# A two-layer decoder trunk with sparse attention on one core: blocks of queries of the first layer taken in the order 4, 5, 6, 7, 2, 3, 1, 0

## The chip, the cores and the metric

The kernel runs on one core of a Trainium2 chip. A core has a matrix engine (TensorE, PE in the profile, with its weight loads listed as PEld), VectorE (DVE), ScalarE (ACT), GpSimd (POOL) and SyncE (SP), which only issues transfers here. Each engine works through its own instructions in a fixed order and waits in place when an operand is not there. The metric is the device time of one execution in microseconds (us).

## The reference, cut to what matters

1,024 tokens of width 1,024 pass through two layers. In each, a modulated layer norm feeds one input projection, whose columns go to two branches: a gated spatial mixing (`u`, `v`, `z_a`) and an attention of 8 heads with one shared key and value, in which a small indexer scores all earlier keys and keeps 256 per query. Both branches go through one output projection, and a layer norm ends the layer.

```python
def hybrid_layer(x, cond, cos, sin, w_ada, b_ada, w_in, ..., w_out, ln_g, ln_b):
    h = layer_norm(x) * (1.0 + scale) + shift
    u, v, z_a, q, k, val, z_b, q_idx, k_idx, w_idx = jnp.split(h @ w_in, SPLIT_POINTS, axis=-1)
    y_a = jax.nn.silu(z_a) * spatial_gating_unit(u, v, v_norm_g, v_norm_b, w_spatial, b_spatial)
    ...
    y_b = jax.nn.silu(z_b) * sparse_attention(q, k, val, q_idx, k_idx, w_idx)
    y = jnp.concatenate([y_a, y_b], axis=-1) @ w_out
    return layer_norm(ALPHA * x + gate * y, ln_g, ln_b)
```

Attention is causal and goes by blocks of 128 queries, numbered 0 to 7. Block i sees (i + 1) x 128 keys at most, so block 7 has eight times the keys of block 0. The blocks do not depend on each other, and each gives 128 rows of the layer's output. The second layer needs all 1,024 rows for its keys, and 512 rows for each half of its projections.

## The kernel before, in words

A layer (`layer`, line 873 on) projects the tokens in two halves of 512, with weights on the sides as products of 128x512. Every float32 product is done as three products of split numbers: an array is split into a high part (ScalarE, L302) and a low part (GpSimd, L303). The list `self.halves` (L882) says which half of the tokens each projection takes first; the second layer takes it from the order of the layer before. After the first projections come the indexer's scores (`scores`, products L528, sums L535), then a bisection on VectorE that finds each query's 256th score (`select`, counting passes L543), interleaved with the other projections and with the spatial gating (`sgu`, L442 and L480, one step for each block of 128 tokens). `u_za` (L488 on) multiplies the gating result by the projected `u` and `z_a` on VectorE (L492), a half at a time.

Attention then runs over steps t = 0 to 15, two for each block (four heads each), in the order `ORDERS[l]` (L73). What stands beside it is bound to the *position* of a block in that order, not to its number:

- Step t: scores of the step (`att_soft`: products L678, VectorE L679, ScalarE exponent L684, GpSimd scaling by the reciprocal L687) and the product with the values of step t - 1 (`att_pv`: transposes L698, split on ScalarE and VectorE L701 and L702, products L703 and L704, sum L710).
- Between these products, `fill` sets products of the output projection (`out_mm`, L740), in pieces of three. 384 of them are in a layer. For positions 0 to 3 (`MERGE`) the gated branch's half (`merge_top`) and the attention's half (`out_bottom`) share an accumulator; for the last four positions the gated half comes early (`out_top` at t = 0, 1, 3, 5, stored in memory), and only the attention's half comes after the block.
- `out_bottom` of position k runs at t = 2k + 3. It ends with a layer norm and, on GpSimd, two passes over 128x1024 (L795, L796); only the last position does these on VectorE (`FAST`).
- The product of the attention with its gate (L712) stands on VectorE, but on GpSimd for blocks 1 and 5 (`ZPB`).
- Toward the next layer: `next_x` (from t = 7), `next_hT` (t = 9 for positions 0 and 1, t = 13 for positions 2 and 3; transposes L272, GpSimd L286), the first weights of the next layer (`first_load`, t = 16, with their splits on GpSimd), and `next_hT` of the last four positions after the loop.

So the number of the block decides only how much attention a step holds: 8 score products of 128x512 or less per four heads and two chunks for the long blocks, and i + 1 transposed groups in `att_pv`.

```python
        for t in range(-1, T + 2):
            ...
            if t >= 3 and t % 2 == 1:
                todo += [self.out_bottom(l, A[order[(t - 3) // 2]], wb, (t - 3) // 2 in self.FAST[l])]
            if t in self.TOPS[l] and self.TOPS[l].index(t) not in self.MERGE[l]:
                todo += [self.out_top(l, order[self.TOPS[l].index(t)], wt)]
            if t >= 2 and t % 2 == 0 and (t - 2) // 2 in self.MERGE[l]:
                todo += [self.merge_top(l, A[order[(t - 2) // 2]], wt)]
            if not last and t in self.NH:
                k = self.NH.index(t)
                todo += [self.next_hT(l + 1, order[k:k + self.NH.count(t)], self.HN)]
```

The order of each engine's instructions is set when the program is built, by a scheduler that moves independent work past each other; what it did is shown in the section on the change.

Of the kernel before, what the change touches and what calls it, by code (L numbers as in the profile page):

```python
# [66 lines left out]
class Trunk:  # L67
# [2 lines left out]
    PACE_SEL = 0.8  # L70
    STEPS = 6
    PTAGS = ('ya', 'w', 'w', 'ya', 'w')
    ORDERS = ((1, 0, 2, 3, 4, 5, 6, 7), (4, 5, 6, 2, 3, 7, 1, 0))  # L73
    PACE = 1.1
    RDVE = 1
    DMOD = ()
# [685 lines left out]
    def bottom_split(self, l, A):  # L762
        A["r"] = self.load_row(self.xin[l] if self.ORDERS[l].index(A["i"]) in self.MERGE[l] else self.r_dram[l], A["i"])
        A["ys"] = self.g("gc", [P, 4, P], F32R), self.g("gc", [P, 4, P], F32R)
        self.split(A["ys"][0], A["ys"][1], A["y"])
# [8 lines left out]
    def out_bottom(self, l, A, w, end):  # L774
        nc = self.nc
        i, r = A["i"], A["r"]
        for nh in range(2):
            acc = yield from self.out_mm(w, A["ys"], nh, A["acc"][nh])
            rv = r[:, nh * 512:(nh + 1) * 512]
            if self.ORDERS[l].index(i) in self.MERGE[l]:  # L780
                nc.vector.scalar_tensor_tensor(rv, rv, ALPHA, acc, op0=ALU.mult, op1=ALU.add)  # L781
# [94 lines left out]
    def layer(self, l, wts):  # L876
# [4 lines left out]
        self.ya = []  # L881
        self.halves = (0, 1) if l == 0 or self.ORDERS[l - 1][0] < 4 else (1, 0)  # L882
        specs = [(C_QI + 256, True, lambda w: self.queries(l, 1, 1, w))]
# [63 lines left out]
        nc.sync.dma_start(self.lb, a["ln_b"][l].partition_broadcast(P))  # L947
        order = self.ORDERS[l]
        steps = [(i, g) for i in order for g in range(2)]
# [111 lines left out]
```

## Time and profile before

| what | us |
|---|---|
| three runs | 1204.15, 1205.03, 1211.92 (median 1205.03) |
| profiled execution | 1208.58, of which the span of the trace is 1206.9 |
| first layer: up to the start of attention | 417 |
| first layer: attention and output projection | 417 to 651 |
| second layer: first projections, scores, rest of the projections | 651 to 993 |
| second layer: attention and output projection | 993 to 1199 |
| busy: PE, DVE, POOL, ACT | 1122.7 (93%), 842.1 (70%), 554.7 (46%), 502.2 (42%) |

The rows below are of the profiled execution. Times are from the start of the span. PEclk is the granted clock of TensorE, as a share of its higher level of 2.4 GHz: 1.00 is that level, 0.50 the lower level of 1.2 GHz. Matmuls overlap, so the busy time of one (some 0.4 us) is more than what it takes of the engine; the chain of work that ended last shows the latter.

### The profile page before, as it was taken

What the parts mean: (1) busy time and instruction counts of PE and PEld (TensorE: products, weight loads), DVE (VectorE), ACT (ScalarE), POOL (GpSimd) and SP (SyncE); (2) the same over time, 40 slices, a digit from 0 to 9 for tenths busy, and PEclk for the clock granted to TensorE, in tenths of its full rate; (3) what the DMA queues carried; (4) which work ended last, traced back from release to release, by engine and by line L of the source; (5) the groups of instructions that cost most, each with busy time, mean ns of one, the idle gap of its engine ahead of it and who ended that gap; (6) DMA issues with size and microseconds to landing.
All of it is one profiled execution on the core that took longest, in us unless ns stands there. A gap on an engine that the chain in (4) does not pass through costs nothing. (4 is left out here: it accounts for less than half of the span.)

```text
span 1206.9 us, 16501 instructions
## 1 busy us (share of the span) xinstructions
PE 1122.7 (93%) x5460; PEld 892.3 (74%) x5460; DVE 842.1 (70%) x1900; ACT 502.2 (42%) x972; POOL 554.7 (46%) x469
## 2 busy tenths in 40 slices
PE   5889999997999989988988999999989998999997
PEld 1467788866878778866766787888677886787885
DVE  6775666999773355688985467589977127878775
ACT  0342355420202454465764435562211136667561
POOL 1563310553323495474766532126323357565653
PEclk9989999998899989999999999999989998999999
DMA  8935721567412574322232474222621246132311
GB/s 264 278 101 179 205 71 36 166 219 257 117 54 79 166 218 158 105 97 62 86 95 74 138 229 123 70 68 88 227 90 45 88 132 202 51 106 88 114 36 61
DMA packets 127057, 152.11 MB, mean 126 GB/s; under 512 B 17396, under 2 KB 94580, under 8 KB 126968
## 3 DMA queue, kind: packets, MB, share of 16 engines
q1 hardware_dynamic: 126968, 151.03, 40.4%
q8 instruction: 43, 0.70, 0.2%
q14 instruction: 46, 0.38, 0.1%
HBM read 111.40 MB, written 35.40 MB: 122 GB/s over the span
## 5 line engine op out<-in xcount | busy, mean ns | idle before, releaser
L349 PE MATMUL pacc<-h,w 128*128 128x512 f32 (+2 forms) x2304 | 548.5, 394 | 10.8 <-DVE ya L492 8.4
L349 PEld LDWEIGHTS pacc<-h,w 128*128 128x128 f32 (+1 forms) x2304 | 427.1, 190 | 106.8 <-DVE ya L492 10.1
L303 POOL TENSOR_TENSOR w<-wr,w 128x512 fp32r<-128x512 f32 (+1 forms) x100 | 133.0, 1345 | 247.7 <-ACT w L302 231.9
L740 PE MATMUL pacc<-h,gc 128*128 128x512 f32 x768 | 196.7, 401 | 10.8 <-ACT gc L302 10.8
L740 PEld LDWEIGHTS pacc<-h,gc 128*128 128x128 f32 x768 | 143.8, 192 | 40.0 <-ACT gc L302 11.9
L302 ACT ACTIVATE w<-wr 128x512 fp32r<-128x512 f32 (+1 forms) x100 | 56.4, 601 | 208.9 <-PE pacc L349 147.0
L535 DVE SCALAR_TENSOR_TENSOR sc<-gc,wi,sc 128x384 f32<-128x384 f32 (+3 forms) x140 | 99.3, 752 | 38.8 <-ACT gc L530 37.0
L678 PE MATMUL ps<-kd,q 128*128 128x512 f32 (+4 forms) x384 | 106.2, 377 | 9.1 <-DVE mx L679 8.8
L702 DVE TENSOR_TENSOR ga<-ppt,ga 128x512 fp32r<-128x512 f32 x144 | 96.6, 684 | 15.5 <-ACT ga L701 14.9
L701 ACT ACTIVATE ga<-ppt 128x512 fp32r<-128x512 f32 x144 | 82.4, 592 | 36.8 <-PE ppt L698 35.9
L368 POOL TENSOR_TENSOR ga<-ga,ga 128x512 fp32r<-128x512 f32 (+2 forms) x40 | 56.9, 1429 | 85.5 <-ACT ga L367 76.8
L678 PEld LDWEIGHTS ps<-kd,q 128*128 128x128 f32 x384 | 65.1, 196 | 26.7 <-DVE mx L679 19.5
L687 POOL TENSOR_SCALAR w<-w,rd 128x256 f32<-128x256 f32 (+6 forms) x77 | 61.3, 799 | 50.7 <-DVE rd L686 32.5
L698 PE MATMUL ppt<-ident,w 128*128 128x128 f32 x349 | 74.9, 276 | 0.0
L239 POOL TENSOR_TENSOR rs<-rs,mhalf 128x1 f32<-128x1 f32 x48 | 34.8, 730 | 81.2 <-DVE rs L238 81.2
L722 DVE TENSOR_TENSOR wr<-wr,r 128x1024 f32<-128x1024 f32 x8 | 12.1, 1508 | 84.6 <-DMA wr<-in_w_out 52.3
L684 ACT ACTIVATE w<-w,mx 128x256 f32<-128x256 f32 (+6 forms) x77 | 60.6, 787 | 23.4 <-DVE mx L679 23.1
L703 PE MATMUL po<-ga,vv 128*128 128x512 f32 x144 | 62.4, 433 | 8.5 <-DVE gb L710 6.7
L543 DVE TENSOR_SCALAR_CACHE_REDUCE junkd<-sc,sv 128x384 int8<-128x384 f32 (+2 forms) x72 | 67.7, 940 | 1.4
L704 PE MATMUL po<-ga,vv 128*128 128x512 f32 x144 | 63.2, 439 | 3.0 <-DVE ga L702 2.9
L530 ACT ACTIVATE gc<-ppt 128x384 f32<-128x384 f32 (+3 forms) x96 | 47.9, 526 | 30.4 <-PE ppt L528 25.8
L199 DVE SCALAR_TENSOR_TENSOR r<-r,cond,r 128x1024 f32<-128x1024 f32 x28 | 41.8, 1494 | 25.4 <-DMA r<-in_w_ada 25.4
(198 smaller groups left out, 1750.5 us busy)
## 6 DMA issues: line engine op xcount, KB each, us to landing
wr<-in_w_in SPq DMA_DIRECT2D x50, 512.0 KB, 4.7
r<-in_w_ada SPq DMA_DIRECT2D x32, 512.0 KB, 4.2
q<-q SPq DMA_DIRECT2D x112, 128.0 KB, 3.2
q<-ga SPq DMA_DIRECT2D x48, 256.0 KB, 3.0
h<-in_w_ada SPq DMA_DIRECT2D x32, 256.0 KB, 5.2
wr<-in_w_out SPq DMA_DIRECT2D x16, 512.0 KB, 4.1
r<-r SPq DMA_DIRECT2D x14, 512.0 KB, 3.9
r<-x SPq DMA_DIRECT2D x12, 512.0 KB, 4.8
```

The costliest lines, as they stand in the source:

```text
L303: self.nc.gpsimd.tensor_tensor(lo, src, hi.bitcast(F32), op=ALU.subtract)
L349: self.nc.tensor.matmul(acc[:m, :tn], w[:, k, :m], h[:, k % 2, t0:t0 + tn], start=(k == 0 and i == 0), stop=(k == NK - 1 and i == 2))
L535: nc.vector.scalar_tensor_tensor(sc[:, c0:c0 + w], r[:, :w], wsc, sc[:, c0:c0 + w], op0=ALU.mult, op1=ALU.add)
L543: self.nc.vector.tensor_scalar(j[:, :n], sc, thr, None, op0=op, op1=ALU.add, accum_out=out)
L678: nc.tensor.matmul(ps[:, :w], q[:, g * 4 + h, :], self.KD[x][:, c0:c0 + w], start=(x == 0), stop=(x == 1))
L687: nc.gpsimd.tensor_scalar(pm[:, :n], pm[:, :n], rd, 0.0, op0=ALU.mult, op1=ALU.add)
L698: nc.tensor.transpose(pt[:, h * P:(h + 1) * P], pr[h][:, kt * P:(kt + 1) * P], self.ident)
L701: nc.scalar.activation(ph, pt, AF.Copy)
L702: nc.vector.tensor_tensor(pl, pt, ph.bitcast(F32), op=ALU.subtract)
L703: nc.tensor.matmul(o, self.V[:, kt, :], ph, start=(kt == 0), stop=False)
L704: nc.tensor.matmul(o, self.V[:, kt, :], pl, start=False, stop=(kt == i))
L740: self.nc.tensor.matmul(acc, s[:, k, :], m[:, cs], start=(first and k == i == 0), stop=(not more and k == 3 and i == 2))
```

## The change

The first layer's order of blocks is turned so that the long ones come first. Everything that is bound to a position stays at its position. Two things follow beside the order itself: `self.halves` of the second layer becomes (1, 0), since the first block of the order is not below 4, so that tokens 512 to 1023 are projected first there; and the last blocks to leave the first layer are 2, 3, 1 and 0, so tokens 0 to 511 are the later ones. The second layer's own order of attention stays. The counts of instructions stay on TensorE, VectorE, ScalarE and GpSimd.

```diff
@@ -70,7 +70,7 @@
     PTAGS = ('ya', 'w', 'w', 'ya', 'w')
-    ORDERS = ((1, 0, 2, 3, 4, 5, 6, 7), (4, 5, 6, 2, 3, 7, 1, 0))
+    ORDERS = ((4, 5, 6, 7, 2, 3, 1, 0), (4, 5, 6, 2, 3, 7, 1, 0))
```

The first place is GpSimd near the end of the first layer's attention. Names with `gc` are splits of an attention result on its way to L740, `ya_2280` and `ya_2282` are weights of the next layer, `r` are rows in the closing norm. Before:

```order
L239 TENSOR_TENSOR rs_2236_7393<-rs_2236_7393,mhalf_5_71 128x1
L239 TENSOR_TENSOR rs_2241_7409<-rs_2241_7409,mhalf_5_71 128x1
L795 TENSOR_TENSOR r_2175_7190<-r_2175_7190,r_1490_4947 128x1024
L303 TENSOR_TENSOR ya_2280_7538<-wr_2277_7533,ya_2279_7537 128x512
L303 TENSOR_TENSOR ya_2280_7538<-wr_2278_7535,ya_2279_7537 128x512
L796 TENSOR_TENSOR r_2175_7190<-r_2175_7190,r_1491_4948 128x1024
L303 TENSOR_TENSOR ya_2282_7544<-wr_2277_7533,ya_2281_7543 128x512
L303 TENSOR_TENSOR ya_2282_7544<-wr_2278_7535,ya_2281_7543 128x512
L303 TENSOR_TENSOR gc_2270_7510<-gb_2127_7046,gc_2269_7509 128x512
```

Now, from the scaling of the last probabilities of block 0 (L687) on:

```order
L687 TENSOR_SCALAR ya_2244_7423<-ya_2244_7423,rd_2249_7436 128x256
L795 TENSOR_TENSOR r_2141_7110<-r_2141_7110,r_1490_4947 128x1024
L712 TENSOR_TENSOR gb_2106_7015<-gb_2106_7015,gb_2105_7013 128x512
L303 TENSOR_TENSOR ya_2280_7538<-wr_2277_7533,ya_2279_7537 128x512
L303 TENSOR_TENSOR ya_2282_7544<-wr_2277_7533,ya_2281_7543 128x512
L796 TENSOR_TENSOR r_2141_7110<-r_2141_7110,r_1491_4948 128x1024
L303 TENSOR_TENSOR ya_2280_7538<-wr_2278_7535,ya_2279_7537 128x512
L303 TENSOR_TENSOR ya_2282_7544<-wr_2278_7535,ya_2281_7543 128x512
L303 TENSOR_TENSOR gc_2223_7363<-gb_2106_7015,gc_2222_7362 128x512
L303 TENSOR_TENSOR w_2369_8064<-wr_2366_8059,w_2368_8063 128x512
L303 TENSOR_TENSOR gc_2270_7510<-gb_2192_7287,gc_2269_7509 128x512
```

The split of the last block (`gc_2270`) is the last of these in both. What is new is that the split of the block before it (`gc_2223`, block 1) has moved behind the weights as well, and its gate product L712 stands on GpSimd ahead of it.

The second place is TensorE at the same point. Now, with block 1's output products (`pacc_2231`, `pacc_2247`) and the last transposes of block 0 (`ppt_2264`):

```order
L698 MATMUL ppt_2264_7491<-ident_4_66,w_2239_7406 128x128
L698 MATMUL ppt_2264_7491<-ident_4_66,ya_2244_7423 128x128
L272 MATMUL ppt_2296_7599<-ident_4_66,q_2224_7366 128x128
L272 MATMUL ppt_2298_7609<-ident_4_66,q_2224_7366 128x128
L272 MATMUL ppt_2300_7619<-ident_4_66,q_2224_7366 128x128
L740 MATMUL pacc_2231_7383<-h_1494_4956,gc_2222_7362 128x512
L740 MATMUL pacc_2231_7383<-h_1495_4957,gc_2222_7362 128x512
L740 MATMUL pacc_2247_7430<-h_1494_4956,gc_2222_7362 128x512
L740 MATMUL pacc_2247_7430<-h_1495_4957,gc_2222_7362 128x512
L703 MATMUL po_2263_7490<-ga_2265_7496,vv_144_599 128x512
L704 MATMUL po_2263_7490<-ga_2266_7497,vv_144_599 128x512
L740 MATMUL pacc_2231_7383<-h_1494_4956,gc_2223_7363 128x512
```

Before, the output products of the block ahead of the last (block 6, `gc_2177`) were over by then, and the last transposes of block 7 stood among transposes for the next layer (L272):

```order
L698 MATMUL ppt_2264_7491<-ident_4_66,w_2195_7241 128x128
L698 MATMUL ppt_2264_7491<-ident_4_66,ya_2201_7259 128x128
L704 MATMUL po_2242_7413<-ga_2260_7475,vv_144_599 128x512
L703 MATMUL po_2242_7413<-ga_2262_7485,vv_144_599 128x512
L272 MATMUL ppt_2296_7599<-ident_4_66,q_2178_7196 128x128
L272 MATMUL ppt_2296_7599<-ident_4_66,q_2238_7402 128x128
```

What moved is the whole of block 1's output projection, 24 products, to a place behind the last attention of the layer, where only the last block's 24 stood before.

The third place is VectorE in the second layer, at the gating (L480, whose four rows are one group of 128 tokens, the last group being `po_2674`) and the first products with `u` (L492, first of `pacc_2733`). Before:

```order
L480 SCALAR_TENSOR_TENSOR ya_2605_9007<-po_2642_9188,vg_2570_8773,bsum_2572_8777 128x128
L543 TENSOR_SCALAR junkd_2651_9232,sv_2603_8976<-sc6_2498_8551,sv_2603_8976 128x896
L243 TENSOR_SCALAR gc_2673_9320<-ppt_2669_9308,mv_2671_9315,rs_2672_9317 128x512
L492 TENSOR_TENSOR ya_2580_8806<-ya_2580_8806,pacc_2733_9707 128x512
L543 TENSOR_SCALAR junkd_2652_9234,sv_2603_8976<-sc7_2532_8654,sv_2603_8976 128x1024
```

Now:

```order
L480 SCALAR_TENSOR_TENSOR ya_2599_8947<-po_2674_9322,vg_2570_8773,bsum_2572_8777 128x128
L480 SCALAR_TENSOR_TENSOR ya_2605_9007<-po_2674_9322,vg_2570_8773,bsum_2572_8777 128x128
L585 TENSOR_SCALAR ps_2607_9034<-sv_2603_8976 128x6
L492 TENSOR_TENSOR ya_2580_8806<-ya_2580_8806,pacc_2733_9707 128x512
L492 TENSOR_TENSOR ya_2586_8866<-ya_2586_8866,pacc_2740_9770 128x512
```

The gating goes through its groups from token 0 up in both. The half of `u` that comes first now belongs to tokens 512 to 1023, so `pacc_2733` is used up only after the eighth group, where it was used up after the fourth.

## Rows read from the trace of the kernel before

**Rows 1.** Stages: us, busy (x instructions) of each engine, PEclk, DMA share, GB/s.
```profile
417.00:589.00 172.00, 158.27 (x779) 127.66 (x778) 126.73 (x358) 98.99 (x202) 106.88 (x96) 0.95 0.40 122
589.00:651.00 62.00, 54.36 (x273) 41.85 (x272) 45.59 (x102) 39.50 (x74) 45.29 (x39) 0.94 0.37 115
993.00:1199.00 206.00, 195.97 (x1005) 158.83 (x1003) 153.64 (x421) 121.08 (x242) 122.08 (x109) 0.98 0.31 96
```

**Rows 2.** Chain that ended last, second layer's attention: start, length in us, what.
```profile
1173.88 0.11 PE ppt L698
...
1175.36 5.48 PE pacc L740 x24
```

**Rows 3.** What TensorE waited for, 417 to 589: us in total, times, longest.
```profile
PE ps L678 <- DVE mx L679: 6.7, 11, 2.1
PE pacc L740 <- ACT gc L302: 3.1, 1, 3.1
```

**Rows 4.** The same view, 589 to 651.
```profile
PE po L703 <- DVE gb L710: 3.1, 2, 1.9
PE pacc L740 <- ACT gc L302: 2.6, 1, 2.6
```

**Rows 5.** The same view, 993 to 1199.
```profile
PE pacc L740 <- ACT gc L302: 5.1, 1, 5.1
```

**Rows 6.** Columns of rows 1, short stretches of the first layer's attention.
```profile
421.50:431.50 10.00, 6.85 (x23) 5.38 (x23) 5.34 (x19) 6.62 (x18) 9.19 (x8) 0.50 0.79 237
440.00:460.00 20.00, 20.00 (x99) 16.96 (x98) 11.73 (x36) 11.16 (x26) 13.90 (x14) 1.00 0.68 214
580.00:600.00 20.00, 18.74 (x101) 14.78 (x100) 19.62 (x46) 15.12 (x28) 16.66 (x14) 1.00 0.25 82
```

**Rows 7.** GpSimd by form, 417 to 651: count | busy us, mean ns | idle before.
```profile
L795 POOL TENSOR_TENSOR r<-r,r 128x1024 f32<-128x1024 f32 x7 | 17.4, 2491 | 4.5 <-ACT r L253 4.3
L796 POOL TENSOR_TENSOR r<-r,r 128x1024 f32<-128x1024 f32 x7 | 16.8, 2394 | 0.1
...
L303 POOL TENSOR_TENSOR gc<-gb,gc 128x512 fp32r<-128x512 f32 x8 | 10.4, 1294 | 7.8 <-ACT gc L302 7.8
...
L239 POOL TENSOR_TENSOR rs<-rs,mhalf 128x1 f32<-128x1 f32 x13 | 7.6, 597 | 5.8 <-DVE rs L238 5.7
...
L687 POOL TENSOR_SCALAR w<-w,rd 128x256 f32<-128x256 f32 x7 | 5.3, 756 | 0.0
L303 POOL TENSOR_TENSOR ya<-wr,ya 128x512 fp32r<-128x512 f32 x4 | 5.0, 1282 | 0.0
...
L687 POOL TENSOR_SCALAR ya<-ya,rd 128x256 f32<-128x256 f32 x6 | 3.8, 641 | 0.0
```

**Rows 8.** GpSimd in time near the tail: start, us, instructions [idle <- releaser].
```profile
605.14 2.81 POOL L795 TENSOR_TENSOR r<-r,r 128x1024 f32<-128x1024 f32 x1 [1.03 <-ACT r L253]
...
625.82 4.34 POOL L303 TENSOR_TENSOR w<-wr,w 128x256 fp32r<-128x256 f32 x6 [7.41 <-PE ppt L698]
...
633.00 2.38 POOL L795 TENSOR_TENSOR r<-r,r 128x1024 f32<-128x1024 f32 x1 [1.81 <-ACT r L253]
```

**Rows 9.** TensorE in time: ends of two out products; second layer's last score.
```profile
595.78 1.29 PE L740 MATMUL pacc<-h,gc 128*128 128x512 f32 x5
...
626.06 1.41 PE L740 MATMUL pacc<-h,gc 128*128 128x512 f32 x5
...
807.85 0.62 PE L528 MATMUL ps<-r,q 128*128 128x512 f32 x2
...
879.50 0.79 PE L349 MATMUL pacc<-h,w 128*128 128x512 f32 x1 [3.36 <-DVE ya L492]
```

**Rows 10.** VectorE in time, second layer: end of the scores.
```profile
813.21 0.17 DVE L557 BATCH_NORM_AGGREGATE smv<-bn 128x2 f32<-128x6 f32 x1
```

**Rows 11.** VectorE's lines, 810 to 880: count | busy us, mean ns | idle before.
```profile
L543 DVE TENSOR_SCALAR_CACHE_REDUCE junkd<-sc,sv 128x384 int8<-128x384 f32 (+5 forms) x24 | 22.5, 936 | 0.2
...
L364 DVE TENSOR_TENSOR ga<-ga,ga 128x512 f32<-128x512 f32 x3 | 2.5, 828 | 0.0
```

## The prediction, made before the changed kernel ran

> **What bounds the kernel now.** I read the stages first [rows 1]. In the first layer's attention, the stretch that the change rearranges, TensorE is busy 158.27 of 172 us and then 54.36 of 62; in the second layer's attention, 195.97 of 206. So TensorE bounds every stage, and the change leaves its counts alone. A new order can then gain or lose only idle time and granted clock. In the first piece these are 13.7 us idle and, at a clock of 0.95, 172 x 0.05 = 8.6 us; in the second, 7.6 and 62 x 0.06 = 3.7. For what an instruction takes of TensorE I went to the chain that ended last: 24 products of 512 columns in 5.48 us, so 0.228 each, and a transpose in 0.11 [rows 2]. Then the waits, stage by stage [rows 3 to 5], and GpSimd, which does the last step ahead of many of them [rows 7, 8].
>
> **The change part by part.** I cut the first layer's attention where the fourth position's output projection ends. In the new order that is block 7 and TensorE's row 2346; what stands ahead (matrix work of the four long blocks with the early output halves) comes to 144 us: 288 L740, 55 each of L703 and L704 at 0.228, 220 L698 and 12 L272 at 0.11, and 148 L678 by width. The first 172 us before hold nearly the same amount, 143.5 us by the same prices, so the two pieces can be compared one to one.
>
> *A, the opening, up to block 7's output products.* Before: 172 us for 143.5, so 28 us lost. Part of this belongs to the start of attention, which stays: in ten microseconds near its beginning the clock is 0.50, so 5.0 us are lost, with the DMA share at 0.79 [rows 6], and the single wait of 3.1 us for the first split [rows 3]. What remains is 13.7 - 3.1 = 10.6 us idle and 8.6 - 5.0 = 3.6 of clock, 14.2 together. The second layer's attention begins with 4, 5, 6 already, and loses there 10.0 - 5.1 [rows 1, 5] idle, or 4.1 for 172 us, and 0.02 x 172 = 3.4 of clock: 7.5. The difference is 14.2 - 7.5 = 6.7; I take **-6**. Bounds: 0 if the waits for VectorE [rows 3] only change place, -12 if nearly all of the 14.2 goes.
>
> *B, the tail: blocks 2 (its end), 3, 1 and 0 with the output products of the last four positions.* TensorE's own price is 44.4 us against 46.9 before, which took 62. But the small blocks have 2 to 4 transposed groups each, so TensorE reaches the end early, and it is GpSimd's fixed order that decides. The last products of block 1 read the low half `gc_2223`, which stands behind everything else on GpSimd. From block 7's first norm pass (L795) to that split, GpSimd has, at the rows' means [rows 7]: 3 pairs of L795 and L796 (2.49 + 2.39), 14.6; 16 scalings L687 of 256 wide at 0.70 (between 0.756 and 0.641), 11.2; 4 passes L286 for the next layer, of 128x512 like the splits and so at 1.29, 5.2; 5 L239 at 0.60, 3.0; 3 splits `gc` at 1.29, 3.9; the 6 small weight splits as one 4.34 piece [rows 8], 4.3; 4 splits `ya` at 1.28, 5.1; and block 1's L712, which has the split's 1.29 by its shape, 1.3. The sum is 48.6. In front of it lies the way from the last product of the bottom to L795: 597.07 to 605.14 is 8.1 and 627.47 to 633.00 is 5.5 [rows 8, 9]; I take 7. Behind it stand the 24 products of block 1, less the four that need only the high half, and the 24 of block 0: 44 x 0.228 = 10.0. GpSimd itself will wait for its inputs; its row shows such a wait of 1.0 and 1.8 us per norm [rows 8], I take 2 in all. While TensorE waits the clock falls, and I take 3.4, near the 3.7 that this stretch lost before. Sum: 7 + 48.6 + 2 + 10.0 + 3.4 = 71.0, against 62, so **+9**. Bounds: at the low end 5.5 for the way, 47 for GpSimd (the 16 scalings at 0.60 or below), no wait, no clock: 62.5, or +0.5. At the high end 8.1 for the way, 8 of waits (a 7.41 us wait stood ahead of the weight splits before [rows 8]), 5 of clock: 79.7, or +17.
>
> What is hidden here at present: before, the long blocks 5, 6 and 7 gave TensorE work through the same stretch, and of the waits that remain, 2.6 us at the last block's split and 3.1 for L710 [rows 4] are the largest. That cover is what the new order uses up early.
>
> *C, the second layer with its later half first.* The keys of the first half are needed for the scores. They come last now, so 225 full products L349 and 29 transposes L272 stand ahead of the first score instead of 182 and 16: 43 x 0.228 + 13 x 0.11 = 11.2 us, and with overlaps 11.5. This work is then missing behind the scores. But VectorE's chain decides there: the product with `u` of the first half (L492 of `pacc_2733`) now belongs to the later tokens, which the gating reaches last, and TensorE cannot refill the accumulator until L492 is done. From the end of the scores (807.85 + 0.62 on TensorE, 813.4 on VectorE [rows 9, 10]: a lag of 5) to the row at 879.50, which waited for L492 [rows 9], VectorE spends 66 us. By the new order 5 counting passes at 0.94, six rotary passes at some 0.83 [rows 11], one product L492 and nine short instructions have slipped behind that row: 4.7 + 5.0, and an estimate of 2 for the rest, leave 54.5. Then 24 products, 5.5, to the same point. So 5 + 54.5 + 5.5 = 65 in place of 71.4 (808.1 to 879.5), and with the 11.5 more ahead: 11.5 + 65 - 71.4 = **+5**. Bounds: 0 if the work shifted ahead is all given back, +9 if VectorE's chain is not shortened by more than 3. From that row on both programs have the same rows, so nothing follows.
>
> The edit of L882 costs nothing by itself. Transfers move with their blocks: the loads of queries and gates are the same in count, one more long block's at the start, where the DMA share is 0.79 [rows 6]; A's opening, taken as it was, holds that.
>
> **Sum.** -6 + 9 + 5 = +8 on the profiled 1208.58 gives 1216.6. That execution is 3.55 above the median of 1205.03, and on the median the sum gives **1213 us**. The forecast's own range is 1207 to 1217.
>
> **The rivals.** *Faster, because two regimes are mixed.* In 440 to 460 TensorE is full and VectorE has 11.73 of 20; in 580 to 600 VectorE has 19.62 of 20 and TensorE loses 1.26 [rows 6]. Long blocks beside the early output halves would level that. Then A is -12, B its low end of +0.5, and C is 0: -11.5, 1194. For it: the waits for L679 total 6.7 in the first piece [rows 3], and the second layer's attention, which starts with long blocks, loses 10.0 us idle in 206 [rows 1], 5.1 of them in one wait [rows 5]. Against it: a tail with little on TensorE to cover GpSimd's queue. The Trainium skill (page Perfetto Trace Analysis, section Optimization Strategy) says that where the most contended engine changes over time, mixing these stretches may improve performance; by that rule alone the change would be a gain. The rows bear it out for the opening and not for the tail. I give it 0.22, of which 0.13 lies beyond 1%.
>
> *Slower: GpSimd's queue at its upper price.* B at +17, A and C as above: +16, 1221. It decides from B = +13 on (-6 + 13 + 5 = +12, 1%), which is 4 us more of waits in the chain from block 7's norm to `gc_2223` than the 2 that I take. For it: every norm waits for ScalarE [rows 8], and three norms stand in a row. Against: GpSimd is busy in 45.29 of the 62 us of that stretch before [rows 1], and does not stand still by nature. Chance 0.33.
>
> *The waits only change place.* A is -6, B +6, C 0, since L492's delay is covered by other products: 1205. Chance 0.10.
>
> **How the numbers follow.** Forecast 0.35, gain 0.22, slower 0.33, no change 0.10. The gain case spreads around its 1194, so a low end of 1196 leaves about half of it out, 0.1; the slow case spreads above its 1221 by some more microseconds of waits, and a high end of 1228 leaves out another 0.1. About 1%, 12 us, is what a measurement of this kernel can tell from no change. Below 1193 lies 0.13, the lower part of the gain; above 1217 the slow case, 0.33; between them the forecast, the third rival and the rest of the gain, 0.54.
>
> **What would show it.** A: the first layer's attention has fewer waits of L678 for L679, and the clock above 0.95 up to block 7's output. B: in the last 25 us ahead of the second layer's first L349, TensorE waits for GpSimd, at L698 for L687 and at L740 for the split `gc` L303, with the clock at 0.50 in places. C: the first L528 comes some 11 us later after the first L349, and one wait of TensorE for L492 of about 10 us stands in the middle of the counting passes; the second layer's attention takes the same 206 us. The prediction is wrong if the tail shows TensorE at work throughout, or if the opening keeps its 28 us.

## The result, and the profile after

The changed kernel took 1223.71 us (median of 4 runs, 1219.17 to 1226.81) against 1204.91 before: a ratio of 1.0134, 95% interval 1.0103 to 1.0165. That is slower, by a little more than 1%. The forecast was 1213, its own range 1207 to 1217; the time lies above that range and inside the wide one (1196 to 1228), nearest to the slow rival's 1221.

The profiled execution after is the fastest of its runs (1219.17, span 1217.5), that of before was above its median, so the two traces differ by 10.6 us where the medians differ by 18.8. The same kernel run again (below) was profiled at 1225.55.

The stages of the trace after, cut as the prediction cuts them (columns as in [rows 1]; the first two answer to its first two rows):

```profile
417.00:577.00 160.00, 151.84 (x774) 123.40 (x773) 116.31 (x313) 94.23 (x178) 90.08 (x76) 0.98 0.35 109
577.00:652.00 75.00, 55.85 (x256) 42.23 (x255) 53.37 (x141) 40.54 (x90) 56.14 (x57) 0.86 0.41 127
...
1004.50:1210.00 205.50, 195.34 (x999) 158.08 (x997) 151.57 (x422) 120.85 (x241) 122.93 (x109) 0.98 0.30 93
```

What TensorE waited for in the opening (417 to 577, columns as in [rows 3]):

```profile
PE pacc L740 <- ACT gc L302: 5.6, 1, 5.6
...
PE ps L678 <- DVE mx L679: 0.6, 2, 0.5
```

The opening got shorter, 160 us for 172, at a clock of 0.98 for 0.95; the wait of L678 for VectorE's L679 is nearly gone, while the single wait for the first split grew from 3.1 to 5.6. The tail got longer, 75 for 62, with TensorE idle for 19 us and the clock at 0.86. The second layer's attention is what it was, 205.5 us.

For all kernels of this study, from the same marks in each trace (us): the opening runs from 417 to the 288th product L740 (before: to 589.2, the same amount of work), the tail from there to the second layer's first product, "second layer" from that to its 785th product L349, from where on the rest is equal. The single profiled execution of a kernel can lie some us off its median; those of descending and before_late_tops are the slowest of twelve. The kernels ran in groups, each with the kernel before beside it, whose median was between 1204.9 and 1207.0; the ratios are to the kernel before of the same group, and differences between kernels of different groups are better read from the ratios.

| kernel | opening | tail | second layer | median | ratio to before (95%) |
|---|---|---|---|---|---|
| before | 172.2 | 62.0 | 234.9 | 1204.91 | |
| changed | 159.6 | 75.7 | 244.6 | 1223.71 | 1.0134 (1.0103 to 1.0165) |
| again | 162.0 | 78.4 | 245.0 | 1223.25 | 1.0125 (1.0089 to 1.0160) |
| gpsimd | 161.2 | 83.6 | 244.5 | 1225.67 | 1.0169 (1.0140 to 1.0198) |
| gating | 160.9 | 78.4 | 239.7 | 1219.69 | 1.0104 (1.0082 to 1.0127) |
| keep | 165.5 | 94.7 | 232.8 | 1231.91 | 1.0201 (1.0176 to 1.0226) |
| gate1 | 162.7 | 74.2 | 244.4 | 1220.21 | 1.0103 (1.0066 to 1.0140) |
| scalar_norm | 163.3 | 74.9 | 241.3 | 1218.03 | 1.0088 (1.0057 to 1.0119) |
| long_last | 158.0 | 77.4 | 243.7 | 1219.38 | 1.0116 (1.0081 to 1.0150) |
| descending | 249.6 together | | 232.8 | 1213.83 | 1.0048 (1.0024 to 1.0073) |
| three | 161.6 | 74.8 | 239.6 | 1216.44 | 1.0090 (1.0058 to 1.0122) |
| two_long_last | 162.8 | 79.5 | 238.9 | 1220.09 | 1.0114 (1.0081 to 1.0147) |
| before_scalar_norm | 236.1 together | | 233.5 | 1204.99 | 0.9998 (0.9974 to 1.0023) |
| before_late_tops | 242.0 together | | 233.5 | 1207.72 | 1.0010 (0.9988 to 1.0032) |

So, in the changed kernel's profile: opening -12.6, tail +13.7, second layer +9.7, in sum +10.8, against 10.6 between the spans.

What TensorE waited for in the tail, 577 to 653 (columns as in [rows 4]):

```profile
PE po L704 <- DVE ga L702: 4.8, 4, 2.8
PE pacc L740 <- POOL gc L303: 4.4, 1, 4.4
PE po L703 <- DVE gb L710: 3.7, 3, 1.8
PE pacc L740 <- ACT gc L302: 2.8, 2, 1.9
PE ppt L272 <- DVE ga L702: 1.9, 1, 1.9
```

The largest single wait is the one that was forecast: the output products of block 1 stand for GpSimd's split. In time, on TensorE at that place:

```profile
633.33 2.08 PE L740 MATMUL pacc<-h,gc 128*128 128x512 f32 x4 [1.89 <-ACT gc L302]
...
640.68 11.74 PE L740 MATMUL pacc<-h,gc 128*128 128x512 f32 x44 [4.42 <-POOL gc L303]
652.26 1.07 PE L349 MATMUL pacc<-h,w 128*128 128x512 f32 x4
```

The four products that need only the high half, then block 0's last two attention products, then 4.4 us of nothing, then the remaining 44 in one piece of 11.7 us. Part of that piece runs at the lower clock: from 640.68 to 645.00 the granted clock was 0.64. And on GpSimd, from the longest of its waits to that split:

```profile
601.85 0.48 POOL L687 TENSOR_SCALAR w<-w,rd 128x256 f32<-128x256 f32 x1 [7.22 <-DVE rd L686]
...
617.94 1.28 POOL L286 TENSOR_TENSOR h<-gc,h 128x512 fp32r<-128x512 f32 x1 [1.50 <-DVE h L283]
...
627.73 2.79 POOL L795 TENSOR_TENSOR r<-r,r 128x1024 f32<-128x1024 f32 x1
630.49 1.26 POOL L712 TENSOR_TENSOR gb<-gb,gb 128x512 f32<-128x512 f32 x1
631.71 2.48 POOL L303 TENSOR_TENSOR ya<-wr,ya 128x512 fp32r<-128x512 f32 x2
634.15 2.36 POOL L796 TENSOR_TENSOR r<-r,r 128x1024 f32<-128x1024 f32 x1
636.48 2.48 POOL L303 TENSOR_TENSOR ya<-wr,ya 128x512 fp32r<-128x512 f32 x2
638.91 1.72 POOL L303 TENSOR_TENSOR gc<-gb,gc 128x512 fp32r<-128x512 f32 x1
```

The line of work ahead of the split is there in the order forecast, without a gap from L795 on. Ahead of it lies one wait of 7.22 us, in which the next scaling of probabilities stands for VectorE's reciprocal (L686); the sum had 2 us for all waits together.

### The profile page after: what moved, and what is told of

The parts are those of the page before. It is cut to its first block, busy times and chain, and to the rows that moved or that the text cites. A ratio compares the mean times of both kernels' runs of the same rounds, so it can differ in the third digit from the quotient of the medians.

```text
span 1217.5 us, 16527 instructions
## 1 busy us (share of the span) xinstructions
PE 1117.0 (92%) x5460; PEld 888.0 (73%) x5460; DVE 845.5 (69%) x1900; ACT 503.2 (41%) x972; POOL 560.4 (46%) x469
## 5 line engine op out<-in xcount | busy, mean ns | idle before, releaser
L349 PE MATMUL pacc<-h,w 128*128 128x512 f32 (+2 forms) x2304 | 546.2, 392 | 10.6 <-DVE ya L492 8.2
L349 PEld LDWEIGHTS pacc<-h,w 128*128 128x128 f32 (+1 forms) x2304 | 423.6, 189 | 105.2 <-DVE ya L492 9.8
L303 POOL TENSOR_TENSOR w<-wr,w 128x512 fp32r<-128x512 f32 (+1 forms) x100 | 134.4, 1360 | 263.5 <-ACT w L302 253.9
L740 PE MATMUL pacc<-h,gc 128*128 128x512 f32 x768 | 199.8, 403 | 17.7 <-ACT gc L302 13.3
L740 PEld LDWEIGHTS pacc<-h,gc 128*128 128x128 f32 x768 | 144.2, 192 | 48.1 <-ACT gc L302 14.4
L678 PE MATMUL ps<-kd,q 128*128 128x384 f32 (+4 forms) x384 | 103.2, 368 | 4.0 <-DVE mx L679 3.4
L368 POOL TENSOR_TENSOR ga<-ga,ga 128x512 fp32r<-128x512 f32 (+2 forms) x40 | 59.7, 1502 | 86.3 <-ACT ga L367 84.9
L687 POOL TENSOR_SCALAR w<-w,rd 128x256 f32<-128x256 f32 (+6 forms) x77 | 62.0, 808 | 55.1 <-DVE rd L686 40.1
L678 PEld LDWEIGHTS ps<-kd,q 128*128 128x128 f32 x384 | 64.6, 192 | 20.1 <-DVE mx L679 12.7
L698 PE MATMUL ppt<-ident,w 128*128 128x128 f32 x349 | 75.3, 275 | 0.0
L704 PE MATMUL po<-ga,vv 128*128 128x512 f32 x144 | 62.7, 435 | 5.9 <-DVE ga L702 5.3
L687 POOL TENSOR_SCALAR ya<-ya,rd 128x256 f32<-128x256 f32 (+6 forms) x51 | 40.7, 798 | 47.9 <-DVE rd L686 40.3
```

The costliest lines, as they stand in the source:

```text
L303: self.nc.gpsimd.tensor_tensor(lo, src, hi.bitcast(F32), op=ALU.subtract)
L349: self.nc.tensor.matmul(acc[:m, :tn], w[:, k, :m], h[:, k % 2, t0:t0 + tn], start=(k == 0 and i == 0), stop=(k == NK - 1 and i == 2))
L678: nc.tensor.matmul(ps[:, :w], q[:, g * 4 + h, :], self.KD[x][:, c0:c0 + w], start=(x == 0), stop=(x == 1))
L687: nc.gpsimd.tensor_scalar(pm[:, :n], pm[:, :n], rd, 0.0, op0=ALU.mult, op1=ALU.add)
L698: nc.tensor.transpose(pt[:, h * P:(h + 1) * P], pr[h][:, kt * P:(kt + 1) * P], self.ident)
L704: nc.tensor.matmul(o, self.V[:, kt, :], pl, start=False, stop=(kt == i))
```

## The experiments

**The changed kernel again (again).** No edit.

> The changed kernel once more, beside the others of this group. Expected: 1219 to 1227 us, and again about 160 us from the start of the first layer's attention to block 7's last output product, about 76 us from there to the second layer's first product, and about 245 us from that to the 785th product L349 of the second layer (before: 172, 62 and 235). If only one profiled execution was so, these three differ by more than 2 us.

Measured: 162.0, 78.4 and 245.0, so opening and tail lie 2.4 and 2.7 us off the first trace, a little over the 2 us allowed. The tail looked different inside. VectorE, at the place where the row of position 4 is normalised for the next layer:

```profile
630.72 12.88 DVE L243 TENSOR_SCALAR q<-q,mv,rs 128x1024 f32<-128x1024 f32 x1 [0.65 <-POOL rs L239]
```

In the changed kernel's first trace the same instruction:

```profile
627.34 0.98 DVE L243 TENSOR_SCALAR q<-q,mv,rs 128x1024 f32<-128x1024 f32 x1 [0.25 <-POOL rs L239]
```

And what TensorE waited for in the tail of the second execution (577 to 660):

```profile
PE ppt L272 <- DVE q L243: 12.0, 1, 12.0
PE po L704 <- DVE ga L702: 4.0, 3, 2.4
```

The same program, and one instruction takes 0.98 us or 12.88, while the whole tail differs by 2.7 us: the 12.0 us wait stands in place of others, such as the 4.4 us for GpSimd's split. The long pass is taken up in scalar_norm and in the last section.

**GpSimd relieved (gpsimd).**

```diff
-    FAST = ((7,), (6, 7))
+    FAST = ((4, 5, 6, 7), (6, 7))
-    ZPB = ((1, 5), (2, 4, 5, 6, 7))
+    ZPB = ((5,), (2, 4, 5, 6, 7))
```

> The changed kernel with GpSimd relieved at the end of the first layer: the closing passes of the positions 4 to 6 (two of 128x1024 each) stand on VectorE (FAST has 4 to 7), and block 1's gate product L712 too. Theory that GpSimd's fixed order sets the tail: two pairs of 2.49 + 2.39 and one 1.29, 11 us, no longer stand ahead of the low half of block 1's split, which then also passes the weight splits; the tail of 76 us loses 8 to 16 us, and the kernel 8 to 14. Rival, the short steps themselves (transposes, split, product, sum, one after the other for blocks with 1 to 4 groups) set the end: the tail stays within 3 us of 76. Second rival, VectorE takes over as the bound: the tail grows.

Measured: not 8 to 14 us faster but 2.4 us slower in the median (the two intervals of the ratio overlap), and a tail of 83.6. The tail's stage row, of this kernel and of the changed one cut alike:

```profile
578.20:661.70 83.50, 63.95 (x267) 46.56 (x266) 62.57 (x155) 37.17 (x88) 49.73 (x51) 0.80 0.39 120
```
```profile
576.60:652.30 75.70, 56.55 (x260) 42.77 (x259) 53.53 (x142) 40.54 (x90) 56.84 (x57) 0.86 0.40 125
```

GpSimd has 7 us less, VectorE 9 more, and the clock fell to 0.80. So GpSimd's order is not the only thing that holds the tail: with the order cleared, the tail grew, which is the second rival's sign. That it grew because VectorE's added work stands in the chain of the short blocks fits these rows but is argued, not shown. The edit changes two engines at once, so it doesn't tell what clearing GpSimd alone gives; gate1 does.

**Block 1's gate product alone (gate1).**

```diff
-    ZPB = ((1, 5), (2, 4, 5, 6, 7))
+    ZPB = ((5,), (2, 4, 5, 6, 7))
```

> The changed kernel with one instruction moved: block 1's gate product L712 on VectorE and no longer on GpSimd. In GpSimd's order the low half of block 1's split then stands straight behind the first norm pass of position 5, ahead of the four weight splits and the second pass, 8 us earlier. Theory that GpSimd's place in line for that split holds TensorE: the wait of L740 for GpSimd (4.4 us in the profiled execution of the changed kernel) goes, block 1's 24 products start 5 to 8 us earlier, and since the last block's split still stands at the end of the line, 2 to 4 us of the tail are gained. Rival, the serial chain through the short blocks: the split is not what is waited for, the tail stays within 2 us.

Measured: median 1220.21, 3 us under the changed kernel; the intervals overlap, so the times alone don't separate the two. The trace does. TensorE in the tail:

```profile
631.51 2.08 PE L740 MATMUL pacc<-h,gc 128*128 128x512 f32 x4 [0.25 <-ACT gc L302]
...
636.73 0.80 PE L703 MATMUL po<-ga,vv 128*128 128x512 f32 x1 [2.50 <-ACT ga L701]
637.32 5.91 PE L740 MATMUL pacc<-h,gc 128*128 128x512 f32 x20
643.07 0.39 PE L704 MATMUL po<-ga,vv 128*128 128x512 f32 x1
...
646.94 7.17 PE L740 MATMUL pacc<-h,gc 128*128 128x512 f32 x24 [3.37 <-ACT gc L302]
653.96 1.30 PE L349 MATMUL pacc<-h,w 128*128 128x512 f32 x5
```

The wait for GpSimd is gone: block 1's products run from 637.3 and not from 640.7 (the trace as a whole is about 3 us later there, so some 6 us are won). But block 0's last attention product L704 now stands behind these 20, and its sum, gate and split follow it one after the other, until 646.9. The 4.4 us wait for GpSimd became waits of 2.5 and 3.4 for the chain of the last block. So the theory's wait went and the products started earlier, but the tail is 74.2, only 1.5 us under the first trace (the long VectorE pass took 0.97 us here, so the two are alike in that), which is the rival's result. The tail looks like several chains of nearly one length, where each released one hands the end to the next.

**The longer of the late blocks last (long_last).**

```diff
-    ORDERS = ((4, 5, 6, 7, 2, 3, 1, 0), (4, 5, 6, 2, 3, 7, 1, 0))
+    ORDERS = ((4, 5, 6, 7, 1, 0, 2, 3), (4, 5, 6, 2, 3, 7, 1, 0))
```

> The changed kernel with the first layer's last four blocks in the order 1, 0, 2, 3 in place of 2, 3, 1, 0, so that the longer of them close the layer. Theory that the tail is long because blocks with one or two groups of keys give TensorE too little beside the serial chain at the very end: the tail (76 to 78 us from block 7's last output product on) loses 4 to 10 us, the kernel as much. Rival, that the short blocks cost the same anywhere: within 2 us. Second rival, GpSimd's queue alone: unchanged, for its work is the same in sum.

Measured: the tail is 77.4, not shorter; the first rival holds. The four short blocks cost the same in either order. The median is 4 us under that of again, but the kernel before was 1 us slower in this group, and the ratios (1.0116 and 1.0125) have intervals that nearly coincide, so no gain is shown. It did not add to the others either (two_long_last, below).

**Gating of the later half first (gating).**

```diff
     def sgu(self, l):
-        for c in range(NB):
+        for c in [h * 4 + b for h in self.halves for b in range(4)]:
```

> The changed kernel with the spatial gating of the second layer taking the later four groups of tokens first, as its projections do. Theory that VectorE's product L492 of the later half, which waits for the eighth group, holds TensorE: the waits for L492 and L480 between the last score and the 785th L349 (8.3 us, and the half clock behind them) shrink, and the time falls by 4 to 7 us. Rival, that the 13 us by which the scores end later are the whole of it: no change within 2 us.

Measured: the second layer's piece fell from 245.0 to 239.7, the median from 1223.25 to 1219.69, 3.6 us, a little under what was expected; the intervals of the ratios overlap. The trace bears the theory out in part. TensorE's waits for L492 and L480 from the last score to the 785th L349 fell from 8.3 to 5.6 us (with 1.3 more for another VectorE line), and that stretch from 74.8 (75.9 in again) to 72.7, so 2 to 3 us. The rest of the gain lies ahead of the last score (167.0 for 169.8 and 169.1), where scalar_norm, which leaves the gating alone, has 166.9; it is not shown to be the gating's. And 239.7 is still 4.8 above before.

**The flip undone (keep).**

```diff
-        self.halves = (0, 1) if l == 0 or self.ORDERS[l - 1][0] < 4 else (1, 0)
+        self.halves = (0, 1)
```

> The changed order, but the second layer projects tokens 0 to 511 first, as before. Theory that the flip is needed and its price is lower than what it avoids: the second layer's first products wait for the norm of the last blocks, TensorE stands still for 12 to 25 us at its start, of which the undone flip gives 9.7 back: 3 to 15 us slower than the changed kernel. Rival, that the flip itself is the loss and the last blocks are there in time: 8 to 10 us faster than the changed kernel.

Measured: 8.7 us slower than the changed kernel. The second layer's piece is back at 232.8, as before or better, but in front of it TensorE stands (577 to 700):

```profile
PE ppt L272 <- DVE q L243: 12.0, 1, 12.0
PE pacc L740 <- POOL gc L303: 4.8, 1, 4.8
```

These 12.0 us are the row of the last block on its way through the norm; the pass L243 itself takes 0.81 us there, so this is not the long pass of again. The flip is needed with this order, and costs less than it avoids.

**The normalising pass on ScalarE (scalar_norm).**

```diff
-            self.rows[b] = self.ln_row(self.load_row(self.xin[l], b, tag), 1)
+            self.rows[b] = self.ln_row(self.load_row(self.xin[l], b, tag), 2 if tag == "q" else 1)
```

> The changed kernel with the normalising pass (L243, 128x1024) of the two rows that positions 4 and 5 hand to the next layer on ScalarE and not on VectorE. In one execution of the changed kernel this pass took 12.9 us on VectorE while GpSimd worked without a gap from 630.7 to 643.1, in another 0.98. Theory that the pass loses a race for something that VectorE and GpSimd share, and then stands until GpSimd's first gap: with the pass elsewhere no VectorE instruction of the tail takes over 4 us, the spread of the times (1214.6 to 1228.4) narrows to under 8 us, and the median falls by 2 to 5. Rival, that the long pass costs nothing because TensorE waits for GpSimd there anyway: no change of the median within 1.5 us.

Measured: median 1218.03, 5.2 us lower, and a spread of 5.4 us (1214.99 to 1220.41) against 13.8 for six runs of the changed kernel, and no VectorE instruction of the tail over 3 us. That is what the theory asks for, but it is not proved. The intervals of the ratios overlap. The kernel called three below has the pass on ScalarE too, and a spread of 4.8; but gating, with the pass on VectorE and 12.90 us long in its trace, spreads over 6.5 us only. And the tails with the long pass (78.4 in again and in gating) and with the short one (75.7) differ by 2.7 us, too little for a spread of 13.8.

**Three edits together (three)** (gating, normalising pass on ScalarE, block 1's gate product on VectorE).

> The changed kernel with the three single edits together: gating of the later tokens first, the normalising pass of positions 4 and 5 on ScalarE, block 1's gate product on VectorE. If the three losses are separate, their gains add: 4 + 5 + 3 = 12 us off the changed kernel's 1223, so 1209 to 1214, with a spread under 8 us. If they hide each other (each release only hands the wait to the next link of one chain), the last two give no more than the larger of them: 1213 to 1217.

Measured: 1216.44, in the range of the second case. The single gains against again were 3.6, 5.2 and 3.0 us, together 6.8; no interval of these ratios is clear of the changed kernel's. The last two hide each other in the tail, which is 74.8, no shorter than with gate1 (74.2) or scalar_norm (74.9) alone.

**Two edits and the longer blocks last (two_long_last).**

> The order 4, 5, 6, 7, 1, 0, 2, 3 with gating of the later tokens first and the normalising pass on ScalarE. If the gain of the longer last blocks (4 us) is of another kind than those two (4 and 5), 1209 to 1213; if it was the same race of the normalising pass, since that pass fell in another place there, 1213 to 1217. The opening stays at 158 to 163 us, and the second layer's 785th L349 near 240 us from its first product.

Measured: 1220.09, outside both ranges. The second layer's piece came out as expected (238.9), the tail at 79.5, with one wait of 4.7 us for the normalising pass, on ScalarE now.

**Each half in descending order (descending).**

```diff
-    ORDERS = ((4, 5, 6, 7, 2, 3, 1, 0), (4, 5, 6, 2, 3, 7, 1, 0))
+    ORDERS = ((3, 2, 1, 0, 7, 6, 5, 4), (4, 5, 6, 2, 3, 7, 1, 0))
```

> The first layer's blocks in the order 3, 2, 1, 0, 7, 6, 5, 4: the halves as before the change, so the second layer starts with tokens 0 to 511, but within each half the long blocks come first. Theory by stages: the second layer is as before (C is 0: 785th L349 some 235 us from its first product); the opening with blocks 3 to 0 beside the early output halves stays near the 28 us lost before, since VectorE's full stretch with blocks 7 and 6 still comes behind it; the tail with blocks 5 and 4 has cover: in all within 6 us of before, 1200 to 1211. Rival, that starting with the short blocks was the loss of the opening: 6 to 10 us faster than before.

Measured: 1213.83, 0.5% slower than before, a little above the theory's range, and far from the rival: starting with the short blocks was not the loss of the opening. The profiled execution is the slowest of its twelve, but shows where this order loses. VectorE and TensorE in the steps of blocks 7 and 6, which have no early products beside them:

```profile
540.00:550.00 10.00, 9.89 (x55) 7.37 (x54) 9.99 (x30) 8.11 (x15) 3.29 (x4) 1.00 0.19 52
550.00:560.00 10.00, 6.95 (x40) 5.16 (x39) 9.61 (x20) 8.98 (x19) 9.57 (x7) 1.00 0.18 52
560.00:570.00 10.00, 8.46 (x52) 6.52 (x51) 8.89 (x22) 6.87 (x13) 7.26 (x7) 1.00 0.59 188
```

VectorE is at 9.99, 9.61 and 8.89 of 10 and TensorE idles up to 3 us in ten.

**The kernel before, with its early products later (before_late_tops).**

```diff
-    TOPS = ((99, 2, 97, 96, 0, 1, 3, 5), (0, 1, 2, 4, 6, 3, 5, 2))
+    TOPS = ((99, 2, 97, 96, 3, 5, 7, 8), (0, 1, 2, 4, 6, 3, 5, 2))
```

> The kernel before with the four early output halves of its long blocks at t = 3, 5, 7, 8 in place of 0, 1, 3, 5: 48 of the 96 products move from the steps of the short blocks toward the first long one. Theory of the opening (in 510 to 590 us VectorE is at 71 of 80 and TensorE loses 9 us idle, since the long blocks have no products left beside them): a part of the 9 us goes, 2 to 5 us faster than before. Rival, that the short blocks need this cover as much where they stand (blocks 1 and 0 open the layer): what is gained there is lost at 430 to 470, and the time is within 2 us of before or up to 6 slower.

Measured: 1.0010, no change. Three stretches of before, and the same of this kernel (columns as in [rows 1]):

```profile
425.00:440.00 15.00, 14.44 (x59) 11.82 (x60) 9.47 (x23) 9.06 (x23) 15.00 (x16) 0.78 0.60 172
440.00:510.00 70.00, 69.59 (x340) 57.97 (x339) 43.05 (x119) 34.32 (x73) 40.03 (x37) 1.00 0.53 158
510.00:590.00 80.00, 70.89 (x364) 55.69 (x364) 71.34 (x200) 52.03 (x99) 47.78 (x43) 0.96 0.19 62
```
```profile
425.00:440.00 15.00, 10.99 (x48) 9.46 (x48) 5.88 (x19) 7.99 (x20) 13.71 (x15) 0.69 0.64 178
440.00:510.00 70.00, 66.19 (x310) 52.84 (x309) 45.68 (x122) 33.69 (x72) 40.38 (x39) 0.98 0.42 133
510.00:590.00 80.00, 73.15 (x381) 58.21 (x380) 68.25 (x192) 49.88 (x94) 48.26 (x43) 0.99 0.29 96
```

From 510 on, 2.3 us of idle time and the clock's fall are won back, and before that 3.5 and 3.4 us are lost (from 417 to 425 this kernel was 2.6 ahead). This fits the rival, that the short blocks need the cover as much; the trace is 8.6 us above the kernel's median, so the amounts are not those of a usual execution. In the changed kernel the same products stand beside long blocks, and the opening keeps TensorE at 65.93 of 67 us from 510 to 577.

**The normalising pass of the kernel before (before_scalar_norm).** The edit of scalar_norm, on the kernel before.

> The kernel before with the normalising pass of positions 4 and 5 on ScalarE and not on VectorE. Its times so far are spread over 1200.8 to 1211.9. If the same race costs it some executions, the upper ones vanish and the median falls to 1202 to 1205; if GpSimd has gaps enough there, since long blocks leave it idle (45 of 62 us busy), nothing changes: 1204 to 1208 with the same spread.

Measured: 1204.99, ratio 0.9998, with the spread unchanged (1200.44 to 1212.73). The pass is not late there: it took 0.80 and 0.81 us in the trace of before. What spreads the times of before is something else, and stays open.

None of the kernels tried is faster than before.

## Why the forecast was too low

**A, the opening: right in kind, too small.** Forecast -6, measured -12.6, beyond the bound of -12. The mis-sized term is what an opening with long blocks still loses beside the start: 7.5 us were taken, from the second layer's attention. Counted the forecast's way it is 2.6 us, 8.2 idle less the 5.6 of the first split's wait, and none of the clock, which was 1.00 from 430 to 577. The waits of L678 for VectorE fell from 6.7 us [rows 3] to 0.6. That it takes both, long blocks and these products, is supported by two controls: long blocks without them leave TensorE idle (descending), and moving 48 of the products from the short blocks toward the first long one gains nothing (before_late_tops).

**B, the tail: right in place and kind, too small.** Forecast +9, measured +13.7, and +16.4 in the second execution. Of the terms, GpSimd's work was nearly right (48.6 forecast; the 56.3 us between the start of block 7's L795 and the end of block 1's split hold 45.9 of work), and so was the way to L795 (7 forecast, 584.28 - 576.97 = 7.3). The products at the end took 11.6 and not 10.0, and these 1.6 are all that the clock's own term of 3.4 became on this path. The mis-sized term is GpSimd's waiting for its inputs: 2 taken, 10.4 measured, of which 7.22 in one wait. TensorE waited for the split L303 as forecast, and never at L698 for L687. The slow rival's condition (4 us more of waits than taken) came true, though not for its reason: it expected the norms to wait for ScalarE, and 8.4 of the 10.4 us are two waits for VectorE's reciprocal L686. Nor had the forecast seen that GpSimd's line is one of several chains of nearly one length: gate1 shows that clearing it gives 1.5 us of tail and 3 us in the medians, since the attention steps of the short blocks, handed from engine to engine with little on TensorE beside them, are nearly as long. The rival that the tail's waits would only change place had the mechanism, though not the size.

**C, the second layer: right in kind, too small.** Forecast +5, measured +9.7. Up to the start of the last score it is 12.9 (11.5 forecast; a wait of 1.4 us of a score for its queries' transfer is as long as the difference). Behind it the forecast's mark is the row that stood at 879.50 before [rows 9]. That row came 71.4 us after the last score's start before and 71.2 after (822.02 to 893.20), so -0.2 where -6.4 was taken. The other -3.0 lie behind the mark, where the forecast said that nothing follows. Stretches of the trace after, and the last of them before (columns as in [rows 1]):

```profile
885.87:893.20 7.33, 7.33 (x25) 5.87 (x25) 6.88 (x20) 0.03 (x1) 0.00 (x0) 0.75 0.16 48
893.20:896.80 3.60, 3.60 (x17) 3.00 (x16) 3.26 (x14) 2.41 (x3) 2.54 (x2) 1.00 0.00 0
```
```profile
879.50:886.10 6.60, 6.59 (x16) 5.17 (x17) 6.12 (x20) 0.00 (x0) 0.00 (x0) 0.54 0.01 3
```

The same 16 products took 6.6 us before, at a granted clock of 0.54, and 3.6 after. The wait for L492 was there, but not as one wait of about 10 us: it came in pieces, with others. TensorE, after, between the last score and the forecast place, and its waits (822 to 932):

```profile
868.69 1.09 PE L442 MATMUL po<-q,gc 128*64 128x128 f32 x16 [1.74 <-DVE ya L480]
871.11 5.74 PE L349 MATMUL pacc<-h,w 128*128 128x512 f32 x24 [1.33 <-DVE ya L492]
...
879.20 1.09 PE L442 MATMUL po<-q,gc 128*64 128x128 f32 x16 [1.32 <-DVE ya L480]
882.35 1.64 PE L442 MATMUL po<-q,gc 128*64 128x128 f32 x16 [2.06 <-DVE ya L480]
885.87 11.34 PE L349 MATMUL pacc<-h,w 128*128 128x512 f32 x41 [1.88 <-DVE ya L492]
```
```profile
PE po L442 <- DVE ya L480: 5.1, 3, 2.1
PE pacc L349 <- DVE ya L492: 3.2, 2, 1.9
PE po L442 <- DMA gc<-in_v_norm_b: 2.6, 1, 2.6
```

The step that failed is the 65 us behind the scores (5 + 54.5 + 5.5), which came out at 7.0 + 56.9 + 7.3. The scores' sums ended 7.0 us after the start of TensorE's last score. VectorE's stretch up to L492, taken without idle time, held 51.4 us of work and 5.0 of waits (1.3 before):

```profile
DVE ps L574 <- POOL sx L565: 1.5, 1, 1.5
DVE ga L359 <- DMA q<-ga: 1.5, 1, 1.5
DVE gc L243 <- POOL rs L239: 1.2, 1, 1.2
DVE ya L480 <- PE po L442: 0.8, 2, 0.4
```

Only the last of these is the turn-taking with TensorE in the gating; most of the 5.0 us is GpSimd and a transfer. And the 24 products behind the wait ran partly at the lower clock (0.75 granted), 7.3 us and not 5.5. That the term as a whole comes from the flip is shown by keep, whose second layer is back at 232.8.

**The sum.** The three terms came out at -12.6, +13.7 and +9.7 where -6, +9 and +5 were taken: +10.8 for +8 in the profiled execution. That the sum is so near is partly luck: A missed by 6.6 us one way, B and C by 4.7 each the other way. The rest of the way to 1223.7 is in no term: the forecast moved 3.55 us down from the profiled execution to the median of before, and the changed kernel's median lies 4.5 above its own profiled execution. The run again was profiled 6.4 us above the first, of which the tail with its long VectorE pass accounts for 2.7 and the opening for 2.4; what else spreads the changed kernel's times stays open.

**The rivals.** The mixing of regimes, which the Trainium skill (Perfetto Trace Analysis, section Optimization Strategy) says may improve performance, did what the rule says in the opening, 12.6 us, and the rule has nothing on what the mix leaves over: the tail of short blocks, unmixed, lost 13.7. The time fell where the prediction had put 0.33, and not in its 0.54 between the two: B came out between its +9 and its bound of +17, and C beyond its bound of +9. What the two have in common is waits in stretches where TensorE has little else to do; that one cause sets both is not shown.

## What to carry to other kernels

When an order puts cover work beside the long steps, ask at once what stands beside the short steps then, and price that tail as several chains, not as the one engine that looks fullest: one of them gave 1.5 to 3 us here, though its split moved up by 8 us in its own queue. A stretch in which engines hand work to each other costs its waits, the waits of the engine waited for, and the lower clock behind some of them; here two such terms came out 4.7 us above their estimates. And a change of an order that moves an operand's half last should carry the consumers' order with it (the gating's here, worth 2 to 3 us behind the scores).

## What the runs showed of the hardware

One VectorE pass of 128x1024 (L243) took 0.81 us in most places, and 12.88 and 12.90 us in the traces of the runs again and gating. In the first of these GpSimd worked from before the pass's start, 630.72, without a gap until 643.05; the pass ended at 643.60. In the changed kernel's first trace the pass came through in 0.98 us beside the same GpSimd instructions, and the L795 behind it took 2.79 us where 2.33 is its time in the other trace. So the two engines seem to shut each other out over this pass, which took 12 us more in one trace than in the other; the tail as a whole was 2.7 us longer. What decides it is not shown: in both traces the pass began within 0.1 us behind the same GpSimd instruction (L687, of some 0.5 us), and got in ahead of the L795 that follows in the one and not in the other. The Trainium skill (SBUF — State Buffer, section Who interferes with whom) says that VectorE and GpSimd share a pair of ports, that some VectorE passes of this kind take it whole, and that whoever issues first holds it for its instruction while the other blocks. The traces agree with the blocking. In gate1 another such pass took 2.74 us beside one GpSimd pass (L796, 2.40 us), which is a wait for one instruction; the trace of again adds that the loser can wait for a run of nine, until GpSimd had nothing ready.
